# Two 64-row score products in turns instead of one 128-row product of stacked copies, in a two-layer trunk step

## The chip, the cores and the metric

The program runs on one core of one Trainium2 chip. The metric is the device time of one execution in microseconds (us). Every time below is such a time, or is read from one profiled execution of the kernel before.

## What is computed

One step of a hybrid trunk with two layers, 1024 features, 512 sample tokens and 128 prompt tokens. Each layer runs three mixers side by side (differential attention, a chunkwise mLSTM, a spatial gate), merges them by gates, and then runs a gated feed-forward network. The change is in the attention. A head has a query and a key of 128 features, which are two halves of 64, and each half has a softmax of its own:

```
q1, q2 = qblk[..., :DA_HD], qblk[..., DA_HD:]          # DA_HD = 64
p1 = softmax(einsum('bhqd,bhkd->bhqk', q1, k1) * scale)
p2 = softmax(einsum('bhqd,bhkd->bhqk', q2, k2) * scale)
o  = einsum('bhqk,bhkv->bhqv', p1 - lam * p2, v)
```

There are four heads. A block is 128 queries. The four sample blocks read 640 keys (512 of the sample, 128 of the cache); the prompt block reads its own 128.

## The kernel before

Activations lie with their features on the 128 partitions and the 640 tokens (`NT`) along the free dimension. A large product is made of pieces of 320 tokens. Each float32 operand of such a product is split exactly into a high and a low part of type float32r, and a product is the sum of three terms: high by high, high by low, low by high (line 129 for most of the kernel). So one column tile of a weight with eight row tiles is 48 products of 128x128 by 128x320. Each product loads its own stationary operand (the rows of PEld) and then streams its columns (the rows of PE).

The scores use another split. `attn_stacks` makes, for each half j of a head, one tile `qs` that holds the high part of q on 64 partitions and the low part on the other 64, a tile `kh` that holds the high part of k twice, and a tile `kl` that holds its low part twice. Then two products over all 128 rows, with `kh` and with `kl`, give the whole sum. `attn_weights` (line 826) does this for a block: for j = 0 four products into one accumulator (two terms, two pieces of 320 keys; line 840), the maximum (line 845), its scaling (846), the exponential (848); then the same for j = 1; then the difference of the two softmaxes (850 to 854). `attn_apply` turns that difference (862), copies it (864), multiplies it by v (869) and takes the result out of PSUM (870 on VectorE, 872 on ScalarE).

The prompt block goes by line 843: one plain float32 product for each half, on 64 partitions. A plain float32 product appears in the profile as two passes.

All accumulators of this part come from one tag of PSUM with two slots (`psM`, tag `ms`): in the order of the program j = 0, j = 1, then the turned weights of the block before (862), then its result (869), and so on. `attn_head` goes through the prompt block and then the four sample blocks, and applies each block after the scores of the next one. The tiles of `attn_stacks` have the tag `st`, with six slots; a head takes all six.

The order of the instructions on each engine is fixed when the program is built, by a planner (`schedule_with_timeline_sim=True`) that works through the instructions by priority. An attention head is traced under `high_priority()`; the products of line 129 that are traced around it (`mlstm_out`, `branch`, the gates) are ordinary work, and stand between the head's instructions on TensorE.

Of the kernel before, what the change touches and what calls it, by code (L numbers as in the profile page):

```python
# [9 lines left out]
F32 = mybir.dt.float32  # L10
# [6 lines left out]
P = 128  # L17
D = 1024
KD = D // P
NS = 512  # L20
# [4 lines left out]
# the token blocks of a half, and the halves' columns by conditioning (sample 0, prompt 1)  # L25
NPARTS = ((0, P), (P, 2 * P), (2 * P, NHALF))
GROUPS = (((0, NHALF, 0),), ((NHALF, NS, 0), (NS, NT, 1)))
# steps of the covering products before a norm's sums and before their broadcast
COVER = (4, 8)
# steps by which the second of two products that share a new norm lags, for each half  # L30
LAG = (2, 6)
# idle products at the start that keep TensorE's clock up
# [9 lines left out]
# output tiles of the mLSTM branch between the attention heads  # L42
FILL_ML = (0, 2, 4, 8)
# slots of the attention branch's gates that are made before the last head is through
AHEAD = ("qk", "qk", "tg", "tg", "hs")
# the hidden tiles that are summed in one go
FFN_PARTS = ((0, 7), (7, 14), (14, 22))

# columns of the per-layer vector pack
V_DAG, V_MLG, V_FB, V_IB, V_SGG = 0, 1, 2, 3, 4  # L50
V_MCW, V_MCB, V_FCW, V_FCB, V_BMOD, NV = 8, 32, 40, 172, 216, 264
# tile order of the feature-major part of w_in
# [4 lines left out]
class Tags:  # L57
    """A pool with a number of slots for each tag."""
# [8 lines left out]
class Trunk:  # L67
# [9 lines left out]
    # ---------------------------------------------------------------- helpers  # L77
    def psA(self):
        """A 640-column product over two banks; its halves are split at token 320."""
        return self.t(self.ps, [P, 1024], F32, "acc", 2)[:, 192:832]  # L80
# [4 lines left out]
    def alt(self):  # L85
        """VectorE and GpSimd in turns, for work that either can do."""
        self.flip += 1
        return self.nc.gpsimd if self.flip % 2 else self.nc.vector

    def weights(self, src, n):  # L90
        """Loads a chunk and splits it exactly into two float32r parts, 512 columns at a time."""
        nc = self.nc
        raw = self.t(self.wp, [P, n], F32, "raw")
        nc.sync.dma_start(raw, src)
        out = []
        for a in range(0, n, 512):
            b = min(a + 512, n)
            hi = self.t(self.wp, [P, b - a], F32R, "whi")
            lo = self.t(self.wp, [P, b - a], F32R, "wlo")
            nc.scalar.copy(hi, raw[:, a:b])  # L100
            self.alt().tensor_sub(lo, raw[:, a:b], hi.bitcast(F32))  # L101
            out.append((hi, lo))
        return out
# [13 lines left out]
    def mm(self, acc, w, k0, xs, halves=(0, 1), ks=None, pin=False):  # L117
        """acc[m, t] = sum_k w[k, m] x[k, t]; w holds the tiles k0.. of len(xs)."""
# [21 lines left out]
    def tm(self, l, kind, xs, evac):  # L140
        """Token-major product with 512 columns of w_in, 256 columns at a time. Blocks that share a bank
        of the accumulator start it once."""
# [27 lines left out]
    # ---------------------------------------------------------------- set-up  # L170
    def consts(self):
# [8 lines left out]
        # silu of the two conditionings, padded to 32 columns  # L180
# [23 lines left out]
    def layer_consts(self, l):  # L204
# [11 lines left out]
        # tensors of the mixers  # L216
# [29 lines left out]
    def mod_part(self, l, sec, c0, width, src, pin=False):  # L246
        """Columns c0.. of one of the six modulation vectors, as [feature, (sample, prompt)]."""
        self.mod_vector(*self.mod_products(l, sec, c0, width, src, pin))

    def mod_products(self, l, sec, c0, width, src, pin=False):  # L250
        """Rows 32 j and 32 j + 1: the parts that every fourth feature tile gives."""
# [42 lines left out]
    # ---------------------------------------------------------------- norms  # L294
    def norm_open(self, l, sec, pool, tag):
        """A norm is made for one half of the tokens, then for the other. Without sec: the final one."""
        return {"l": l, "sec": sec, "pool": pool, "tag": tag, "acc": [None, None], "u": {}}

    def feed(self, st, k, x, s):
        """Sums the squares of half s of feature tile k, and scales it."""  # L300
# [15 lines left out]
        if k == KD - 2 and s == 0:  # L316
            # has the square root's table in place when the sum is ready
            nc.scalar.activation(self.t(self.sp, [P, 1], F32, "warm", 1), sq[:, 0:1], AF.Sqrt)

    def norm_sums(self, st, s):  # L320
        """The means of squares of half s, as columns in PSUM; the inverse roots."""
# [12 lines left out]
    def norm_bcast(self, st):  # L334
        """The inverse roots on every partition, in PSUM."""
# [7 lines left out]
    def norm_tiles(self, st, s, out):  # L343
        """Half s of the normed tiles, in two parts, added to out."""
# [37 lines left out]
    def start(self, p0):  # L382
        """The first norm, and two products that begin with the half of its features that is there first."""
# [12 lines left out]
        def warm(n):  # L396
            """Keeps TensorE's clock up while it waits."""
# [51 lines left out]
    def handoff(self, srcs, xs, x, g, st, nexts):  # L449
        """The last two tiles of a residual product, the norm that follows, and the first two products with  # L450
        its result, first for one half of the tokens, then for the other: a half's norm is made while
        TensorE works on the other half."""
# [11 lines left out]
        def cover(accs, ws, xs, half, s, order):  # L464
            """Half of the columns of two products, within them the sums of the norm's half s."""
# [22 lines left out]
        # the second product starts some steps later: its accumulator is the last to be free  # L488
# [13 lines left out]
    # ---------------------------------------------------------------- spatial gating  # L502
# [43 lines left out]
    # ---------------------------------------------------------------- mLSTM  # L546
    def mlstm_in(self, l, h):
        """The gates, and v with a column of ones (token-major)."""
# [27 lines left out]
    def gates(self, l, acc):  # L576
        """Rows: forward heads at partitions 0-3, backward ones at 32-35."""
# [10 lines left out]
        # log sigmoid(f) = min(f, 0) - log(1 + exp(-|f|))  # L588
# [14 lines left out]
        # M: running maximum of a chunk's a and of the exponent of the state it starts from (mp)  # L603
# [54 lines left out]
    def mlstm_head(self, l, h, q, k, v, rows, sums):  # L658
        """Both directions of one head over all chunks."""
# [14 lines left out]
        for d in range(2):  # L674
# [15 lines left out]
            # q scaled by what is left of the incoming state, and that state's decay  # L690
# [42 lines left out]
    def head_norm(self, hs, sums):  # L733
        """RMS over each head's width: the inverse for every (token, head)."""
# [25 lines left out]
    # ---------------------------------------------------------------- attention  # L760
# [14 lines left out]
    def attn_qk(self, l, h, head):  # L775
        """Rotated q and k of the sample; the prompt's are left as they are."""
# [16 lines left out]
    def attn_stacks(self, h, q, k):  # L793
        """For both halves j of a head, over all 128 rows: q's high and low part on top of each other,
        and k's high part twice, and k's low part twice (512 keys of the sample, 128 of the cache).
        Then [qh; ql] . [kh; kh] + [qh; ql] . [kl; kl] is the whole product."""
        nc, p = self.nc, self.p1
        out = []
        for j in range(2):
            a, b = slice(HD * j, HD * j + HD), slice(HD - HD * j, P - HD * j)  # L800
            qs, kh, kl = (self.t(p, [P, NT], F32R, "st") for _ in range(3))
            nc.scalar.copy(qs[a, 0:NS], q[a, 0:NS])
            nc.vector.tensor_sub(qs[b, 0:NS], q[a, 0:NS], qs[a, 0:NS].bitcast(F32))
            for src, c0, c1 in ((k[a, 0:NS], 0, NS), (self.ck[a, h, :], NS, NT)):
                nc.scalar.copy(kh[a, c0:c1], src)
                nc.vector.tensor_sub(kl[a, c0:c1], src, kh[a, c0:c1].bitcast(F32))
            nc.vector.tensor_copy(kh[b, :], kh[a, :].bitcast(F32))
            nc.gpsimd.tensor_copy(kl[b, :], kl[a, :].bitcast(F32))
            out.append((qs, kh, kl))
        return out  # L810

    def attn_head(self, l, h, q, k, v, sums):
        """One head: the weights of a block of queries are made while the block before it is applied."""
        nc, p = self.nc, self.p1
        stacks = self.attn_stacks(h, q, k)
        o = self.t(p, [P, NB, P], F32, "hs")
        before = None
        for b in (NB - 1, 0, 1, 2, 3):
            e = self.attn_weights(b, stacks, q, k)
# [6 lines left out]
    def attn_weights(self, b, stacks, q, k):  # L826
# [6 lines left out]
        es = []  # L833
        for j in range(2):
            ps = self.psM()[:, 192:832]
            if sample:
                st, kh, kl = stacks[j]
                for i, kk in enumerate((kh, kl)):
                    for s in (0, 320):
                        nc.tensor.matmul(ps[:, s : s + 320], st[:, qs], kk[:, s : s + 320], start=i == 0, stop=i == 1)  # L840
            else:
                r = slice(HD * j, HD * (j + 1))
                nc.tensor.matmul(ps[:, 0:P], q[r, qs], k[r, NS:NT], start=True, stop=True)
            mx = self.t(self.sp, [P, 1], F32, "mx", 6)
# [33 lines left out]
    # ---------------------------------------------------------------- branches  # L878
# [6 lines left out]
    def branch(self, l, n, h, ys, merged, ms, first=False, last=False, ahead=None):  # L885
        """merged += (1 + tanh(gate / 2)) * (y @ w_branch[n]), twice the gated sum, for output tiles ms."""
# [20 lines left out]
    # ---------------------------------------------------------------- FFN  # L907
    def ffn(self, l, h, accs, x, p2, nxt):
        """The residual update and the next norm."""
# [26 lines left out]
        for f0, f1 in FFN_PARTS:  # L936
            # the next part's first tile fills the time in which this part's last one is finished
# [20 lines left out]
    # ---------------------------------------------------------------- all of it  # L958
# [82 lines left out]
# ---------------------------------------------------------------------- host  # L1041
def _shape_constants():
    """Identity, masks, selectors and rotary tables: they depend on shapes alone."""
# [18 lines left out]
def _tiles(w):  # L1062
    """[L, K, M] -> [L, M/128, 128, K/128 * 128]: one column tile per chunk."""
# [4 lines left out]
def _columns(v):  # L1068
    """[L, n * 128] -> [L, 128, n]."""
# [72 lines left out]
```

## Time and profile before

| what | value |
|---|---|
| median of 3 timed runs | 2445.26 us (2442.68 to 2446.33) |
| the profiled execution, from its first to its last instruction | 2439.1 us |
| what the median holds beyond that span | 6.2 us |
| TensorE matmuls busy | 2408.0 us, 99% |
| TensorE weight loads busy | 2313.9 us, 95% |
| VectorE, ScalarE, GpSimd busy | 1134.0, 944.8, 669.9 us |
| mean granted TensorE clock | 0.998 of full speed |
| products of line 840 | 256 |

The profile gives for the profiled execution its span and no other time. "Busy" of a matmul runs from its start to a modelled end, and one matmul starts before the one ahead of it ends; so the busy time of a group says less than the distance from start to start, which the chain of waits gives as the time of a piece divided by its count. The chain is followed back from the last instruction; each piece names an engine, a tile, a line and how many instructions it holds.

### The profile page before, as it was taken

The numbers are of one execution on the slowest core, as the hardware profiler recorded it, in microseconds if no ns is written. First come the engines' busy times: TensorE is split into PE (matmuls) and PEld (weight loads), VectorE is DVE, ScalarE is ACT, GpSimd is POOL, SyncE is SP. The second block draws the span as 40 slices with busy tenths as digits, with TensorE's granted clock in tenths as the row PEclk, the third lists the DMA queues.
The fourth block names the chain that finished last, engine by engine and source line by source line (L and its number), as shares of the span: only waits on it lengthen the run. The fifth ranks groups of instructions, "written<-read, shape, count | busy, mean of one in ns | idle before, by whom it ended". The sixth has DMA issues, their size and how long they took to land.

```text
span 2439.1 us, 40662 instructions
## 1 busy us (share of the span) xinstructions
PE 2408.0 (99%) x16708; PEld 2313.9 (95%) x16708; DVE 1134.0 (46%) x2111; ACT 944.8 (39%) x1728; POOL 669.9 (27%) x486
## 2 busy tenths in 40 slices
PE   8999999999999999999999999999999999999998
PEld 7999999999598999999999999999986989999998
DVE  5455545553146433424446455455532454244344
ACT  4433335544145322323454332455442543232334
POOL 2322232332222322313213222323322223232231
PEclk9999999999999999999999999999999999999999
DMA  8221221123544234222322212211233432222222
GB/s 282 74 73 64 65 78 62 60 72 132 173 147 160 69 109 140 72 75 79 103 80 70 74 64 66 76 54 62 97 114 120 147 96 74 79 74 73 81 72 69
DMA packets 88761, 227.39 MB, mean 93 GB/s; under 512 B 9472, under 2 KB 23936, under 8 KB 88576
## 3 DMA queue, kind: packets, MB, share of 16 engines
q1 hardware_dynamic: 88576, 224.80, 28.2%
q8 instruction: 131, 2.15, 0.4%
q14 instruction: 54, 0.44, 0.1%
HBM read 217.41 MB, written 7.35 MB: 92 GB/s over the span
## 4 chain that ended last, share of the span: by engine, by line
PE 96%; DVE 3%; ACT 1%; DMA 0%; issue 0%; SPq 0%; DVEq 0%; POOL 0%; POOLq 0%; ACTq 0%
PE acc L129 77%; PE acc L156 6%; PE ms L264 3%; PE ms L869 2%; PE ms L840 2%; PE ms L156 1%; PE ms L862 1%; PE ms L716 1%; PE ms L718 1%; PE ms L705 1%; DVE x L439 0%; PE ms L670 0%; PE ms L536 0%; PE ms L277 0%; PE ms L327 0%
## 5 line engine op out<-in xcount | busy, mean ns | idle before, releaser
L129 PE MATMUL acc<-h,whi 128*128 128x320 f32 x6464 | 1246.9, 311 | 5.0 <-DVE h L356 3.3
L129 PEld LDWEIGHTS acc<-h,whi 128*128 128x128 f32 x6464 | 1019.3, 188 | 32.1 <-issue 19.3
L100 ACT CAST whi<-raw 128x512 fp32r<-128x512 f32 x596 | 365.3, 614 | 1038.1 <-PE acc L129 787.9
L101 POOL TENSOR_TENSOR wlo<-raw,whi 128x512 fp32r<-128x512 f32 (+1 forms) x298 | 390.7, 1311 | 1355.1 <-ACT whi L100 1304.7
L129 PE MATMUL acc<-h,wlo 128*128 128x320 f32 x3232 | 755.4, 310 | 0.0
L129 PEld LDWEIGHTS acc<-h,wlo 128*128 128x128 f32 x3232 | 544.2, 188 | 3.5 <-issue 3.4
L101 DVE TENSOR_TENSOR wlo<-raw,whi 128x512 fp32r<-128x512 f32 (+1 forms) x298 | 241.2, 810 | 451.0 <-ACT whi L100 435.0
L129 PE MATMUL acc<-act,whi 128*128 128x320 f32 x1408 | 269.6, 310 | 0.0
L129 PEld LDWEIGHTS acc<-act,whi 128*128 128x128 f32 x1408 | 222.0, 188 | 4.2 <-issue 2.5
L129 PE MATMUL acc<-act,wlo 128*128 128x320 f32 x704 | 165.5, 309 | 0.0
L129 PE MATMUL acc<-y,whi 128*128 128x320 f32 x768 | 154.3, 314 | 1.7 <-DVE y L114 1.7
L499 DVE SCALAR_TENSOR_TENSOR x<-acc,mod,x 128x128 f32<-128x128 f32 (+3 forms) x136 | 66.3, 527 | 181.3 <-PE acc L129 181.3
L165 DVE SCALAR_TENSOR_TENSOR cw<-acc,vec,cw 128x511 f32<-128x511 f32 (+1 forms) x176 | 95.7, 544 | 115.1 <-ACT cw L163 114.0
L156 PE MATMUL acc<-whi,h 128*128 128x256 f32 x768 | 145.7, 283 | 0.0
L129 PEld LDWEIGHTS acc<-y,whi 128*128 128x128 f32 x768 | 121.2, 188 | 17.3 <-issue 11.7
L156 PEld LDWEIGHTS acc<-whi,h 128*128 128x128 f32 x768 | 123.0, 192 | 0.0
L129 PEld LDWEIGHTS acc<-act,wlo 128*128 128x128 f32 x704 | 119.1, 188 | 0.0
L916 POOL TENSOR_TENSOR cw<-cw,cw 128x640 f32<-128x640 f32 x44 | 69.2, 1573 | 156.5 <-DVE cw L167 151.9
L156 PE MATMUL acc<-wlo,h 128*128 128x256 f32 x384 | 108.7, 283 | 0.0
L167 DVE SCALAR_TENSOR_TENSOR cw<-acc,vec,cw 128x511 f32<-128x511 f32 (+1 forms) x176 | 96.7, 550 | 6.0
L129 PE MATMUL acc<-y,wlo 128*128 128x320 f32 x384 | 92.1, 315 | 0.0
L848 ACT ACTIVATE wk<-ms,mx 128x640 f32<-128x640 f32 (+1 forms) x80 | 56.7, 709 | 76.6 <-DVE mx L846 73.2
(257 smaller groups left out, 2425.0 us busy)
## 6 DMA issues: line engine op xcount, KB each, us to landing
raw<-w_in_f SPq DMA_DIRECT2D x98, 512.0 KB, 3.4
raw<-w_up SPq DMA_DIRECT2D x88, 512.0 KB, 3.3
wk<-w_mod SPq DMA_DIRECT2D x72, 256.0 KB, 3.4
mw<-w_mod SPq DMA_DIRECT2D x72, 256.0 KB, 5.7
raw<-w_down SPq DMA_DIRECT2D x32, 448.0 KB, 3.3
raw<-w_in_v SPq DMA_DIRECT2D x24, 512.0 KB, 3.7
raw<-w_branch SPq DMA_DIRECT2D x24, 512.0 KB, 3.3
mw<-w_mod SPq DMA_DIRECT2D x16, 512.0 KB, 8.8
```

Source lines behind the costliest of these rows:

```text
L100: nc.scalar.copy(hi, raw[:, a:b])
L101: self.alt().tensor_sub(lo, raw[:, a:b], hi.bitcast(F32))
L129: ins = nc.tensor.matmul(acc[:, s], a[:, sl], b[:, s], start=k == 0 and i == 0, stop=k == last and i == 2)
L156: nc.tensor.matmul(accs[b], a[:, bs], w[:, sl], start=first and b % 2 == 0, stop=last and (b % 2 == 1 or b == NB - 1))
L165: nc.vector.scalar_tensor_tensor(dst[:, a + 1 : b], acc[:, a : b - 1], w0, dst[:, a + 1 : b], ALU.mult, ALU.add)
L167: nc.vector.scalar_tensor_tensor(dst[:, a : b - 1], acc[:, a + 1 : b], w2, dst[:, a : b - 1], ALU.mult, ALU.add)
L264: ins = nc.tensor.matmul(ps[j : j + 32, 0:width], self.cs[:, k, :], raws[k], start=k < 4, stop=k >= 4, tile_position=(0, j))
L499: self.nc.vector.scalar_tensor_tensor(x[:, a:b], acc[:, a:b], g[:, k, i : i + 1], x[:, a:b], ALU.mult, ALU.add)
L840: nc.tensor.matmul(ps[:, s : s + 320], st[:, qs], kk[:, s : s + 320], start=i == 0, stop=i == 1)
L848: nc.scalar.activation(e[:, 0:nk], ps[:, 0:nk], AF.Exp, bias=mx, scale=scale, accum_out=sm[:, j : j + 1])
L869: nc.tensor.matmul(po, at[:, c * P : (c + 1) * P], vv, start=c == 0, stop=c == n - 1)
L916: nc.gpsimd.tensor_mul(cs[0], cs[0], cs[1])
```

## The change

`attn_stacks` is replaced by `attn_parts`, which splits q and k of a head once, with both halves in place on their own 64 partitions: four tiles `qh`, `ql`, `kh`, `kl` instead of six, and six instructions instead of sixteen. `attn_weights` takes both accumulators of a sample block first and then makes twelve products of 64 rows: three terms, two pieces of 320 keys, and for each of these j = 0 (partitions 0 to 63) and j = 1 (partitions 64 to 127) in turns. The maxima and exponentials of the two halves follow after that. The rest of the diff removes comments and docstrings.

```
-    def attn_stacks(self, h, q, k):
+    def attn_parts(self, h, q, k):
         nc, p = self.nc, self.p1
-        out = []
-        for j in range(2):
-            a, b = slice(HD * j, HD * j + HD), slice(HD - HD * j, P - HD * j)
-            qs, kh, kl = (self.t(p, [P, NT], F32R, "st") for _ in range(3))
-            nc.scalar.copy(qs[a, 0:NS], q[a, 0:NS])
-            nc.vector.tensor_sub(qs[b, 0:NS], q[a, 0:NS], qs[a, 0:NS].bitcast(F32))
-            for src, c0, c1 in ((k[a, 0:NS], 0, NS), (self.ck[a, h, :], NS, NT)):
-                nc.scalar.copy(kh[a, c0:c1], src)
-                nc.vector.tensor_sub(kl[a, c0:c1], src, kh[a, c0:c1].bitcast(F32))
-            nc.vector.tensor_copy(kh[b, :], kh[a, :].bitcast(F32))
-            nc.gpsimd.tensor_copy(kl[b, :], kl[a, :].bitcast(F32))
-            out.append((qs, kh, kl))
-        return out
+        qh, ql, kh, kl = (self.t(p, [P, NT], F32R, "st") for _ in range(4))
+        nc.scalar.copy(kh[:, 0:NS], k[:, 0:NS])
+        nc.scalar.copy(qh[:, 0:NS], q[:, 0:NS])
+        nc.scalar.copy(kh[:, NS:NT], self.ck[:, h, :])
+        nc.vector.tensor_sub(kl[:, 0:NS], k[:, 0:NS], kh[:, 0:NS].bitcast(F32))
+        nc.vector.tensor_sub(ql[:, 0:NS], q[:, 0:NS], qh[:, 0:NS].bitcast(F32))
+        nc.gpsimd.tensor_sub(kl[:, NS:NT], self.ck[:, h, :], kh[:, NS:NT].bitcast(F32))
+        return qh, ql, kh, kl
...
-        es = []
-        for j in range(2):
-            ps = self.psM()[:, 192:832]
-            if sample:
-                st, kh, kl = stacks[j]
-                for i, kk in enumerate((kh, kl)):
-                    for s in (0, 320):
-                        nc.tensor.matmul(ps[:, s : s + 320], st[:, qs], kk[:, s : s + 320], start=i == 0, stop=i == 1)
-            else:
+        pss = [self.psM()[:, 192:832] for _ in range(2)]
+        if sample:
+            qh, ql, kh, kl = parts
+            for i, (x, y) in enumerate(((qh, kh), (qh, kl), (ql, kh))):
+                for s in (0, 320):
+                    for j, ps in enumerate(pss):
+                        r = slice(HD * j, HD * (j + 1))
+                        nc.tensor.matmul(ps[:, s : s + 320], x[r, qs], y[r, s : s + 320], start=i == 0, stop=i == 2)
+        else:
+            for j, ps in enumerate(pss):
                 r = slice(HD * j, HD * (j + 1))
                 nc.tensor.matmul(ps[:, 0:P], q[r, qs], k[r, NS:NT], start=True, stop=True)
+        es = []
+        for j, ps in enumerate(pss):
             mx = self.t(self.sp, [P, 1], F32, "mx", 6)
```

## Rows read from the trace of the kernel before

**Rows 1.** The page: span, TensorE's busy time, the chain by line.

```profile
span 2439.1 us, 40662 instructions
...
PE 2408.0 (99%) x16708; PEld 2313.9 (95%) x16708; DVE 1134.0 (46%) x2111; ACT 944.8 (39%) x1728; POOL 669.9 (27%) x486
...
PE acc L129 77%; PE acc L156 6%; PE ms L264 3%; PE ms L869 2%; PE ms L840 2%; PE ms L156 1%; PE ms L862 1%; PE ms L716 1%; PE ms L718 1%; PE ms L705 1%; DVE x L439 0%; PE ms L670 0%; PE ms L536 0%; PE ms L277 0%; PE ms L327 0%
```

**Rows 2.** Groups of instructions, shapes apart: the scores' products (busy, mean ns).

```profile
L840 PE MATMUL ms<-st,st 128*128 128x320 f32 x256 | 52.0, 319 | 2.4 <-DVE st L807 2.3
```

**Rows 3.** The chain, a long unbroken piece (start us, us, what xcount).

```profile
340.04 17.62 PE acc L129 x120
```

**Rows 4.** The chain in a sample block of the first head, and in the last block.

```profile
392.79 1.12 PE ms L869 x10
393.91 0.59 PE ms L840 x4
394.50 4.10 PE acc L129 x28
398.60 0.58 PE ms L840 x4
399.18 1.17 PE acc L129 x8
...
1780.92 0.59 PE ms L840 x4
1781.51 3.08 PE acc L129 x21
1784.59 0.58 PE ms L840 x4
```

**Rows 5.** Timeline of VectorE and ScalarE behind the first of these blocks.

```profile
394.14 0.28 DVE L870 COPY hs<-ms 128x128 f32<-128x128 f32 x1
...
395.00 0.26 ACT L872 ACTIVATE osq<-ms 128x128 f32<-128x128 f32 x1
395.15 0.19 ACT L872 ACTIVATION_READ_ACCUMULATOR osq<-ms 128x1 f32 x1
```

**Rows 6.** The chain from the prompt block of the second head.

```profile
416.43 0.42 PE ms L843 x4
416.85 5.33 PE acc L129 x35
422.18 0.30 PE ms L840 x2
422.48 1.32 PE acc L129 x9
423.80 0.58 PE ms L840 x4
424.38 1.90 PE acc L129 x13
426.29 0.30 PE ms L840 x2
```

**Rows 7.** The chain from the prompt block of the third head.

```profile
471.70 0.22 PE ms L869 x2
471.93 0.42 PE ms L843 x2
472.34 1.09 PE ms L869 x8
473.43 5.28 PE acc L129 x36
478.71 0.42 PE ms L843 x2
479.13 0.78 PE acc L129 x4
```

**Rows 8.** Lines 843 and 869: durations ns min/median/max, first and last start.

```profile
L843 PE MATMUL ms<-qk,qk x32: 272/322/373, 358.0 to 1745.4; 64*128 64x128 f32 x32
...
L869 PE MATMUL ms<-lc,wk x64: 275/275/275, 383.1 to 1797.3; 128*128 128x128 f32 x64
```

**Rows 9.** The first head: TensorE's busy time in 358 to 416; two timeline rows.

```profile
358.00:416.00 58.00, 56.82 (x407) 56.16 (x407) 34.93 (x70) 33.04 (x70) 12.91 (x10) 1.00 0.16 52
...
362.37 0.56 PE L840 MATMUL ms<-st,st 128*128 128x320 f32 x2
...
364.06 0.83 PE L840 MATMUL ms<-st,st 128*128 128x320 f32 x4 [1.14 <-DVE st L807]
```

**Rows 10.** Lines of `attn_stacks` on VectorE and GpSimd: durations ns min/median/max.

```profile
L803 DVE TENSOR_TENSOR st<-qk,st x16: 685/906/1095, 352.2 to 1743.8; 64x512 fp32r<-64x512 f32 x16
...
L806 DVE TENSOR_TENSOR st<-qk,st x16: 671/686/1660, 360.2 to 1744.9; 64x512 fp32r<-64x512 f32 x16
...
L807 DVE CAST st<-st x16: 486/488/492, 360.9 to 1746.8; 64x640 fp32r<-64x640 f32 x16
...
L808 POOL CAST st<-st x16: 714/964/1043, 361.0 to 1746.9; 64x640 fp32r<-64x640 f32 x16
```

More of the change, by code (lines that the diff above doesn't have):

```diff
@@ L791, in attn_qk @@
         return qk
-    def attn_stacks(self, h, q, k):
+    def attn_parts(self, h, q, k):
         nc, p = self.nc, self.p1
-        out = []
-        for j in range(2):
-            a, b = slice(HD * j, HD * j + HD), slice(HD - HD * j, P - HD * j)
-            qs, kh, kl = (self.t(p, [P, NT], F32R, "st") for _ in range(3))
-            nc.scalar.copy(qs[a, 0:NS], q[a, 0:NS])
-            nc.vector.tensor_sub(qs[b, 0:NS], q[a, 0:NS], qs[a, 0:NS].bitcast(F32))
-            for src, c0, c1 in ((k[a, 0:NS], 0, NS), (self.ck[a, h, :], NS, NT)):
-                nc.scalar.copy(kh[a, c0:c1], src)
-                nc.vector.tensor_sub(kl[a, c0:c1], src, kh[a, c0:c1].bitcast(F32))
-            nc.vector.tensor_copy(kh[b, :], kh[a, :].bitcast(F32))
-            nc.gpsimd.tensor_copy(kl[b, :], kl[a, :].bitcast(F32))
-            out.append((qs, kh, kl))
-        return out
+        qh, ql, kh, kl = (self.t(p, [P, NT], F32R, "st") for _ in range(4))
[6 more added lines that the diff above has]
+        return qh, ql, kh, kl
     def attn_head(self, l, h, q, k, v, sums):
         nc, p = self.nc, self.p1
-        stacks = self.attn_stacks(h, q, k)
+        parts = self.attn_parts(h, q, k)
         o = self.t(p, [P, NB, P], F32, "hs")
@@ L818, in attn_head @@
         for b in (NB - 1, 0, 1, 2, 3):
-            e = self.attn_weights(b, stacks, q, k)
+            e = self.attn_weights(b, parts, q, k)
             if before is not None:
@@ L824, in attn_head, with attn_weights @@
         return o
-    def attn_weights(self, b, stacks, q, k):
+    def attn_weights(self, b, parts, q, k):
         nc, p = self.nc, self.p1
```

## Prediction

> **What bounds the kernel now.** I read the page first, then the groups of instructions, then the chain of waits through the attention, and last the timeline of single instructions. TensorE is busy for 99% of the span, and nearly the whole chain is TensorE's, three quarters of it line 129 [rows 1]. So what counts is the time that TensorE's own sequence takes; what VectorE, ScalarE or GpSimd save pays only where TensorE waits for them. The price of a product is read from an unbroken piece of the chain: 120 products in 17.62 us, 0.147 us from start to start for 320 columns [rows 3]. (The mean of 319 ns in [rows 2] is the modelled length of one, and overlaps its neighbours.) Line 840 pays the same, four in 0.59 us [rows 4]. Its 256 products are 256 x 0.147 = 37.6 us of the span; this is all that the change can touch on TensorE.
>
> **Where the scores stand in TensorE's order.** In a sample block the four products for j = 0 come right behind the block before's line 869; then come 28 products of line 129; only then the four for j = 1 [rows 4]. This pattern, two groups with other work between them, holds for blocks 1 to 3 of all eight heads (24 blocks; j = 1 comes 4.7 us behind j = 0 in the first shown and 3.7 in the last). The reason is the two slots of `ms`. The slot for j = 0 is the one that line 864 has emptied; the slot for j = 1 is that of line 869's result, which lines 870 and 872 empty some time after 869 ends (at about 395.3, 1.4 us after 393.91 [rows 4, 5]). The planner does not let TensorE stand for it: it takes the next instruction that is ready, whatever its place in the program. Its own picture of that release is later still, since j = 1 stands at 398.60.
>
> **What 64-row products cost.** The kernel has some already, line 843. In the second head both halves stand side by side: four passes take 0.42 us of the chain [rows 6]. In the third head they stand apart, and the two passes of one half alone take 0.42 us as well [rows 7]. So a partner in the other half of the array is free, and a half alone is paid in full. A pass itself is no cheaper for having 64 rows: 272 ns recorded for those that don't wait, 275 for a 128-row pass of line 869 [rows 8]. But two passes of 869 take 0.22 us, so 0.20 of the 0.42 is not product. And what follows is long too: eight passes of 869 take 1.09 us where ten take 1.12 (0.20 too much), 35 products of line 129 take 5.33 where 35 x 0.147 = 5.13 (0.20 too much), four take 0.78 for 0.59 [rows 4, 6, 7]. Going from 128-row to 64-row products and back costs about 0.40 us, for each group, in all the places I looked at.
>
> The Trainium skill has this rule on the page "TensorEngine Tiling (Array Packing)", Key Properties: changing the tiling mode, not just the tile, drains TensorE. The trace agrees, and adds the price of 0.40 us that the page doesn't give; without such a price the sum below would be 27 us lower.
>
> **The change part by part.**
>
> Removed: 256 products, -37.6 us.
>
> Added: 384 products of 64 rows by 320 columns in one pass. None is in the trace; from below each costs 0.073 us (every one with a partner), from above 0.147 (alone). The text puts the halves in turns, but what the planner sees is which of them is ready. In blocks 1 to 3, when j = 0's slot is free, j = 1's isn't; the next instruction that is ready is j = 0's second piece, and so on through all six. They need 0.88 us, less than the 1.4 us until the other slot is empty even as the chip runs. So I take two groups of six alone: 12 x 0.147 = 1.76 us in place of 1.17, +0.59 a block. In block 0 both slots come free together if line 843's two halves stood together, which they do in the first two heads of each layer [rows 6] and don't in the other two [rows 7]. So 4 blocks pair (6 x 0.147 = 0.88) and 28 don't (1.76): 3.5 + 49.3 - 37.6 = +15.2 us.
>
> Added: the way in and out, 0.40 us for each group. Blocks 1 to 3 have two groups: 48. Block 0 now comes in three or four pieces, as its operands get ready [rows 6]; this was free among 128-row products and no longer is. I take two for the paired ones and three for the others, since the operands come from six instructions: 4 x 2 + 4 x 3 = 20. 68 x 0.40 = +27.2 us. The bounds: 32 groups (one a block) is 12.8, 88 (five in each block 0) is 35.2; and if only what is lost behind a group counted, 0.20 each, 68 are 13.6.
>
> The preparation: per head VectorE loses two each of lines 803, 806 (twice) and 807, and gains two subtractions over 128 partitions with the same 512 columns, which I take at line 803's 0.9 us; about 3.4 us saved, and GpSimd has a subtraction of 128 columns in place of two copies of 0.96 [rows 10]. Nearly all is hidden already: TensorE idles only 1.18 us of the first head's 58 us, waiting for line 807 between 362.9 and 364.06 [rows 9]. That can go, in both layers: -2.4 us. If it didn't, the cost is those 2.4. GpSimd's piece of `kl` may come late and split a group: counted above.
>
> The later maximum of j = 0, by up to a microsecond, moves line 862 back; line 129's products fill the place, as they do now.
>
> Sum: 15.2 + 27.2 - 2.4 = +40.0 us. The span of 2439.1 becomes 2479.1; with the 6.2 us that the median holds beyond it, 2485 us.
>
> **The rivals.**
>
> *The halves do pair.* The planner might get both slots at one time, if the copy out of 869 counts as short. Then 32 x 0.88 - 37.6 = -9.4 us; groups 24 + 16 = 40, +16.0; idle -2.4: +4.2 us, 2449. For it: line 843 pairs in two heads of four, though nothing in the text asks for it. Against it: 24 blocks in which j = 1 stands microseconds later. 18%.
>
> *Apart, but the change of shape is cheap for these products* (a float32r product streams in one pass, line 843 takes two): 15.2 - 2.4 = +13 us, 2458, or up to 2472 with half the price. Against it: the 0.20 us behind a group falls on 129's one-pass products. 8%.
>
> *Faster: paired, with the shape changed for less.* A paired block saves 0.29 us of products, so the change wins as soon as way in and out cost less than 0.29 us a block in one group. At nothing: -9.4 - 2.4 = -12 us, 2433. Against it are all groups of [rows 6, 7]. 6%. The same page's section Theoretical Speedup gives up to 2x for products of at most 64 rows; taken alone it leads to this time. The trace agrees on the 2x within a pair.
>
> *More pieces than I count*, five and more in each block 0, or groups broken in blocks 1 to 3 too: with 88 groups, no pairs and no idle time regained 15.2 + 3.5 + 35.2 = +54 us, 2499 and more. 6%.
>
> **How the numbers follow.** The forecast, halves apart at 0.40 us a group, has 62%; its own range is 2478 to 2496 (50 to 88 groups, the idle time regained at the one end and not at the other). The time predicted is 2485 us. For 8 in 10 the range also takes in the cheap change of shape and the upper half of the paired case: 2449 to 2499. What a measurement of this kernel can tell from no change is about 0.2%, 4.9 us: "same" is 2440.4 to 2450.2. Half of the paired case lies there: 0.10 with a little of the others. Faster has 0.07, slower 0.83.
>
> **What would show it.** In the chain of the changed kernel: the products of 64 rows in groups of six behind line 869, with some 20 of line 129 before the next six, right if so; groups of twelve that take about 1.1 us would prove me wrong on the order. A group of six should take 1.08 us of the chain (0.88 + 0.20) and the work behind it 0.20 more than its products. TensorE's pause at 363 should shrink. The prediction is wrong if the groups number nearer 32 than 68, if the price of a group is not near 0.40 us, or if a partner is not free for products of 320 columns.

## The result and the profile after

The changed kernel takes 2483.01 us (median of four runs, 2480.61 to 2485.47) against 2445.44 us before (four runs, 2442.68 to 2446.33): a ratio of 1.0158, 95% interval 1.0144 to 1.0173, or 37.6 us more. 2485 was predicted.

The page of the changed kernel (span, busy time of each engine) shows the same kind of kernel as before: TensorE is busy for 99% of the span [rows 1]. TensorE has 128 more products, and VectorE, ScalarE and GpSimd have a little less to do, which buys about 2 us (below).

```profile
span 2483.7 us, 40806 instructions
...
PE 2453.7 (99%) x16836; PEld 2338.7 (94%) x16836; DVE 1114.6 (45%) x2063; ACT 935.7 (38%) x1704; POOL 660.6 (27%) x478
```

The line numbers have moved: the scores' products are line 835 (840 before), the prompt's 839 (843), the transposes 860 (862), the product with the values 867 (869). The groups of instructions, shapes apart, show the new products (busy, mean ns | idle time before them); their mean length is that of the 128-row products [rows 2]:

```profile
L835 PE MATMUL ms<-st,st 64*128 64x320 f32 x384 | 69.9, 324 | 0.0
```

The chain of the changed kernel (start us, us, what xcount): the piece of 120 products that opens the attention, two sample blocks of the first head, and the end of the first layer's attention.

```profile
343.76 17.62 PE acc L129 x120
...
398.28 1.12 PE ms L867 x10
399.39 1.07 PE ms L835 x6
400.46 3.57 PE acc L129 x23
404.03 1.09 PE ms L835 x6
405.12 1.66 PE acc L129 x10
...
602.34 18.18 PE acc L129 x124
620.52 1.98 PE ms L264 x16
```

This is the pattern that the prediction described, beside [rows 4]: two groups of six, apart, 23 products of line 129 between them. Six products would take 0.88 us at 0.147; each group takes 1.07 or 1.09, so 0.20 more. The 23 products behind the first take 3.57 instead of 3.38, the 10 behind the second 1.66 instead of 1.47: 0.19 more each.

The piece of 120 products takes 17.62 us in both kernels [rows 3], and it opens the attention in both, so the stage can be measured from it to the first products of line 264, the modulation behind the attention: 620.52 - 343.76 = 276.76 us here. Before, the same two marks stand at 340.04 and 598.25, 258.21 us:

```profile
598.25 1.98 PE ms L264 x16
```

The second layer shows the same two lengths within 0.1 us. So the attention has grown by 18.55 us a layer, 37.1 us in all, which is nearly the whole of the measured 37.6.

The profiled spans differ by more, 44.6 us. The execution profiled after the change was the longest of its four, and it had a few stretches with the clock at half that the one before didn't have; the windows (stretch, length, busy time of each engine, granted clock, DMA share, GB/s) show one of them, 8 us at 0.57 behind the second attention, where before has 1.00:

```profile
1994.00:2002.00 8.00, 7.75 (x35) 7.37 (x39) 5.86 (x17) 3.26 (x9) 0.00 (x0) 0.57 0.21 66
```

### The profile page after: what moved, and what is told of

Its sections match the earlier page's. It is cut to its first block, busy times and chain, and to the rows that moved or that the text cites. A ratio compares the mean times of both kernels' runs of the same rounds, so it can differ in the third digit from the quotient of the medians.

```text
span 2483.7 us, 40806 instructions
## 1 busy us (share of the span) xinstructions
PE 2453.7 (99%) x16836; PEld 2338.7 (94%) x16836; DVE 1114.6 (45%) x2063; ACT 935.7 (38%) x1704; POOL 660.6 (27%) x478
## 4 chain that ended last, share of the span: by engine, by line
PE 96%; DVE 2%; ACT 1%; issue 0%; DMA 0%; SPq 0%; POOL 0%; DVEq 0%; ACTq 0%; POOLq 0%
PE acc L129 77%; PE acc L156 6%; PE ms L264 3%; PE ms L835 3%; PE ms L867 2%; PE ms L156 1%; PE ms L860 1%; PE ms L716 1%; PE ms L718 1%; PE ms L705 1%; PE ms L670 0%; PE ms L536 0%; PE ms L277 0%; PE ms L327 0%; DVE x L439 0%
## 5 line engine op out<-in xcount | busy, mean ns | idle before, releaser
L843 DVE TENSOR_REDUCE mx<-ms 128x1 f32<-128x640 f32 (+1 forms) x80 | 56.5, 715 | 80.0 <-PE ms L835 79.8
```

Of the source, the lines that this page charges most:

```text
L843: nc.vector.tensor_reduce(mx, ps[:, 0:nk], axis=AX.X, op=ALU.max)
```

## The experiments

The theory (T) is that of the prediction: products that stand apart, plus some 0.40 us for every group that changes the shape of the products, both on TensorE's own sequence. The rivals (R) are named in each expectation. For each kernel the table has the median, the ratio to the kernel before with its interval, and the first layer's attention, measured in the trace from the start of the last product of the values (line 156) to the start of the first of line 264. The marks used above give 0.2 us less. Between these marks lie 1392 products of line 129 in each of the eight kernels, so the stage holds the same other work in all. Each ratio is to the runs of the kernel before that were taken for it; their median is 2445.44 us for the changed kernel, 2443.75 for the next three and for the prompt scores, 2442.71 for the other two.

| kernel | us | ratio | attention, us |
|---|---|---|---|
| before | 2445.44 | | 258.43 |
| after | 2483.01 | 1.0158 [1.0144, 1.0173] | 276.97 |
| products of 128 rows, twelve a block | 2460.25 | 1.0069 [1.0055, 1.0083] | 266.07 |
| products of 128 rows, eight a block | 2444.53 | 0.9999 [0.9990, 1.0007] | 257.33 |
| both accumulators awaited | 2500.29 | 1.0236 [1.0222, 1.0250] | 284.09 |
| awaited in one head only | 2475.98 | 1.0137 [1.0121, 1.0152] | 270.49 |
| before, prompt scores of 128 rows | 2442.48 | 0.9997 [0.9988, 1.0006] | 257.87 |
| before, modulation not split | 2409.27 | 0.9866 [0.9846, 0.9886] | 258.43 |

**The shape alone.** The changed kernel, with its products over all 128 rows; the order of the instructions on each engine stays (in the traces only one spot in the third head differs, where the first two of a block stand in turns with the prompt's passes in the changed kernel).

```
-  nc.tensor.matmul(ps[:, s : s + 320], x[r, qs], y[r, s : s + 320], start=i == 0, stop=i == 2)
+  nc.tensor.matmul(ps[:, s : s + 320], x[:, qs], y[:, s : s + 320], start=i == 0, stop=i == 2)
```

> The changed kernel with one thing undone: the twelve products of a block read all 128 rows of q and k instead of 64 (so each half's scores get the other half's added, which leaves the arithmetic wrong and the work the same in count, order and columns). The instructions stand in the same order on every engine. If the price lies in the change of the array's shape, about 62 groups lose about 0.39 us each (-24.4 us), and the four blocks that ran in pairs lose their partners (+3.5 us): about 2462 us. If the price lies in the number of products and in their weight loads, and the shape is free, nothing is saved and the pairs are lost: 2483 to 2487 us.

2460.25 us. The chain of this kernel in the same two blocks:

```profile
394.38 1.12 PE ms L867 x10
395.49 0.88 PE ms L835 x6
396.37 3.37 PE acc L129 x23
399.74 0.88 PE ms L835 x6
400.62 1.46 PE acc L129 x10
```

Same order, same counts, and all four surcharges are gone: 0.88 instead of 1.07 and 1.09, 3.37 instead of 3.57, 1.46 instead of 1.66. The attention is 10.9 us a layer shorter, 21.8 in all. Two blocks a layer that pair in the changed kernel (below) can't pair here and pay 0.88 more each, 3.5 us. And a wait of the changed kernel, in the first head of each layer, is not in this one (who waits for whom: us in all, times, longest us):

```profile
PE acc L129 <- ACT tg L754: 0.9, 2, 0.5
```

So the shape costs 21.8 + 3.5 - 0.9 = 24.4 us over 62 groups, 0.39 us each. The rival, that groups standing apart are the whole price, falls.

**The preparation alone.** The kernel of the last experiment with eight products a block instead of twelve, as many as before. What is left of the change is its preparation and the order in the text.

```
-  for i, (x, y) in enumerate(((qh, kh), (qh, kl), (ql, kh))):
+  for i, (x, y) in enumerate(((qh, kh), (ql, kl))):
 ...
-  nc.tensor.matmul(ps[:, s : s + 320], x[:, qs], y[:, s : s + 320], start=i == 0, stop=i == 2)
+  nc.tensor.matmul(ps[:, s : s + 320], x[:, qs], y[:, s : s + 320], start=i == 0, stop=i == 1)
```

> As the run before, with two terms instead of three (high by high and low by low, over all 128 rows; the cross terms are left out): eight products of 128 rows a block, as many as the kernel before had, but with the changed preparation, both accumulators taken first, and both maxima behind all products. If these changes beside the products cost nothing, the time is that of the kernel before less some of TensorE's idle time at the first head: 2443 to 2446 us. If the preparation or the later maximum cost anything, it shows here alone: above 2450 us.

2444.53 us, no difference that can be measured from before, and its chain is that of [rows 4] again, with four products in 0.59 us:

```profile
394.56 0.59 PE ms L835 x4
...
399.10 0.58 PE ms L835 x4
```

The attention is 1.1 us a layer shorter than before, so the lighter preparation and the later maximum together give 2.2 us. Of this 1.6 us is idle time of TensorE in the first head: 1.18 us a layer before [rows 9], 0.39 here. Between this kernel and the last lie 64 products a layer and 8.74 us; the last has no idle time there, so the products cost 9.13 us, 0.143 each, where 0.147 was reckoned.

**Pairs forced.** The changed kernel, but the first product of a block waits until the last result has been copied and squared out of its accumulator, so that both accumulators are free when the six of the first half begin.

```
+  def after_evac(self, ins):
+      dep = mybir.DependencyInfo(mybir.DependencyClass.Sync, mybir.DependencyReason.DATA)
+      for e in self.evac:
+          self.tc.add_manual_dep(ins.ins, e.ins.name, dep, reason="both slots")
+      self.evac = ()
 ...
-  nc.tensor.matmul(ps[:, s : s + 320], x[r, qs], y[r, s : s + 320], start=i == 0, stop=i == 2)
+  ins = nc.tensor.matmul(ps[:, s : s + 320], x[r, qs], y[r, s : s + 320], start=i == 0, stop=i == 2)
+  self.after_evac(ins)
 ...
-  nc.vector.tensor_copy(o[:, b, :], po)
+  cp = nc.vector.tensor_copy(o[:, b, :], po)
 ...
+  self.evac = (cp, sq)
```

> The changed kernel, where the first product of a block also waits until the results of the block before have been taken out of PSUM, so that both accumulators are free at once. In the order that is built, all 32 blocks are one group of twelve and the prompt's products one pair. If a partner is free for products of 320 columns, a group takes 1.08 us of the chain and TensorE's own work comes to that of the kernel before within 2 us. But a block's softmax no longer runs beside the other half's wait, the heads take more of line 129's products as cover, and none are left between the last three blocks of each layer's last head: TensorE will stand there for some 3 us a block, about 20 us in all, so 2458 to 2475 us. If products of 320 columns didn't overlap, a group would take 1.96 us and the time be above 2485 us.

2500.29 us, slower than the changed kernel: a miss. All 32 blocks now stand in one group of twelve, and the pairing itself is real. The chain of this kernel (its added lines shift the scores to 842, the product with the values to 875, the transposes to 868) in a block of the first head, and in the last head:

```profile
377.29 1.07 PE ms L842 x12
...
590.70 1.19 PE ms L842 x11
...
597.20 2.52 PE ms L875 x10
...
599.74 0.30 DVE hs L876
...
600.06 0.38 ACT osq L878 x2
...
600.48 2.01 PE ms L842 x12
602.49 1.54 DVE mx L851 x2
...
607.80 2.52 PE ms L875 x10
```

Twelve products take 1.07 us, as long as six alone: the partner costs nothing. But the wait lasts, and other products must fill it. In the last head none are left. Result, copy, square, scores and maximum then follow each other in the chain without a product of line 129 between them, and one block's ten passes of line 875 (five products) come 10.6 us behind the last block's (597.20, 607.80). The windows of this kernel there (same columns):

```profile
589.00:625.00 36.00, 20.54 (x101) 17.05 (x100) 10.61 (x26) 12.48 (x29) 0.00 (x0) 0.56 0.22 66
```

TensorE is busy for 20.5 of 36 us, and the granted clock is 0.56: once TensorE had begun to stand, the clock fell to its lower level (1.2 GHz) for most of this stretch. The chain prices it: the scores take 1.19 us at 590.70 and 2.01 at 600.48, and ten passes of line 875 take 2.52 us, where the same ten took 1.12 in the changed kernel. The expectation had the cover run out at about 3 us a block; a block without cover took 10.6 us, of which its own products at full clock are 2.7 (1.07 scores, 1.12 values, 0.55 transposes), so some 8 are lost. Pairs were tested here together with a wait, so the time says nothing against pairs.

**Pairs in one head.** The same wait, in the third head of each layer only, where products of line 129 are left to fill it.

```
+  self.wait = h == 2
 ...
-  for e in self.evac:
+  for e in self.evac if self.wait else ():
```

> The changed kernel with the wait for both accumulators in the third head of each layer alone. In the order that is built, that head's four sample blocks are one group of twelve each and its prompt products one pair, 5 groups in place of 11, and enough of line 129's products are left to cover it. Four blocks less 0.88 us of products and six groups less at 0.40 us: -5.9 us a layer. The attention of a layer, from the last product of its values to the first modulation product behind it, goes from 277.0 to about 271 us, and the time from 2483 to about 2471 us. If pairing gave nothing, or the waits cost as much as they did with all heads waiting, it stays at 2483 us or above.

2475.98 us, where about 2471 was expected. The chain of this kernel in two blocks of that head (scores line 844, values 877), and just behind the attention:

```profile
488.69 1.07 PE ms L844 x11
...
502.61 1.07 PE ms L844 x11
...
610.20 1.13 PE ms L877 x10
...
612.13 1.28 ACT L738
...
614.82 1.88 DVE hs L741
```

(The chain lists eleven of the twelve; the timeline has all.) In the attention the wait gives 6.5 us a layer, 13 in all, a little more than the 5.9 a layer expected: in the fourth head, too, the first group of scores now follows the prompt's products at once, one group less. In this head pairs do pay, since they also stop its first block from falling to pieces. But the covering products were spent there. Behind the attention 8 of line 129 are left, where the changed kernel has 124 (its chain at 602.34): ScalarE and VectorE appear in the chain, TensorE waits for the norm and the next products' operands, and the stretch between the two attentions is 4.3 us longer than after. By the two medians 7 us of 13 remain; by the distance from the kernel before, 37.6 us after and 33.3 here, only 4. The kernel is still 33 us slower than before.

**The old kernel's own shape change.** The kernel before computes its prompt scores with 64-row products, line 843. Here they have 128 rows, from a tile that holds one half of the keys and zeros in the other.

```
+  self.kz = self.t(lp, [P, 2, P], F32, "kz", 1)
+  nc.gpsimd.memset(self.kz, 0.0)
 ...
+  nc.gpsimd.tensor_copy(self.kz[r, j, :], x[r, NS:NT])
 ...
-  nc.tensor.matmul(ps[:, 0:P], q[r, qs], k[r, NS:NT], start=True, stop=True)
+  nc.tensor.matmul(ps[:, 0:P], q[:, qs], self.kz[:, j, :], start=True, stop=True)
```

> The kernel before, with its only 64-row products (the prompt block's scores) made 128-row ones: the keys of a half with zeros in the other half's rows. If each group of 64-row products costs 0.40 us beside its products, eight lone halves save 0.40 us each and four pairs 0.18 us each (they lose the partner): -3.9 us, about 2441.5 us. If the shape is free: four pairs lose 0.22 us each, 2446 us.

2442.48 us, no measurable difference; the attention is 0.56 us a layer shorter where 1.95 was expected. The waits of TensorE's weight loads over the whole kernel (who waits for whom: us in all, times, longest us):

```profile
PEld ms L845 <- ACT wk L852: 3.0, 6, 0.6
PEld acc L129 <- ACT tg L756: 2.9, 4, 0.8
```

Before, the waits that answer to these two come to 0.6 us in two cases (for line 848) and 2.7 in two (for line 754), so there are six more waits and 2.6 us more of waiting. Of these 2.6 us 0.5 stand in the first heads of the two layers and the rest in the third and fourth, where the kernel before has no such wait. TensorE's own idle time in the attention has grown by 0.5 us a layer, from 1.18 to 1.67. So waiting is a part, perhaps the most, of what lacks of the 3.9 us expected for both layers, of which 1.1 came. The order moved with the edit, so the waits can't be put down to one part of it, and this run is inconclusive.

**Where the kernel before splits its groups.** If each group in another shape is paid for its way in and out, such a group should not be split. Line 264 has such products: eight to a result, four at a time in four 32-column strips of the array, two passes each, so that a whole result is an x16 in the chain. The planner splits them. In the chain of the kernel before, behind the attention:

```profile
612.49 1.85 PE ms L264 x16
...
618.49 0.97 PE ms L264 x2
619.46 0.34 PE acc L129
...
625.21 0.98 PE ms L264 x4
```

One product standing alone (x2) costs 0.97 us, two side by side (x4) 0.98, and all eight in one piece (x16) 1.85. Here the products of a 512-column section are issued in reverse order of their weights, so that the product whose weights land last comes first, and the other seven are ready behind it.

```
-  for k in range(KD):
+  back = width == 512
+  for k in reversed(range(KD)) if back else range(KD):
 ...
-  start=k < 4, stop=k >= 4,
+  start=(k >= 4) == back, stop=(k < 4) == back,
```

> The kernel before, with the other place in which products of a part of the array are split up: the modulation products (line 264, 32 columns wide, four of them side by side in the array) take their eight loads in reverse, so that the first product waits for the last load and the eight stand together. Behind the first layer's attention 26 of these now go in 23 groups, 0.97 us and 0.19 us behind each for lone ones; together eight take 1.85 us and 0.19. That is 26.7 us against 6.6, -20 us for the layer and about as much for the second: 2405 us. What the loads then hold up (11.6 MB pass in this stretch) would take a part of it back: 2405 to 2430 us. If lone products cost only their columns, nothing is gained: 2444 us or more, since the first product waits longer.

2409.27 us, 33 us faster than the kernel before and 74 faster than the changed one. The chain of this kernel (line 265 is the others' 264):

```profile
615.47 1.85 PE ms L265 x16
...
621.48 4.40 PE acc L129 x30
625.88 1.85 PE ms L265 x16
```

Single products with line 129 between them have become whole results of 1.85 us. The attention itself keeps its 258.43 us; the stretch between the attentions is 14.2 us shorter, the one behind the second 16.9, of the 20 expected for each. By the expectation's own sum most of this comes from the partners that a lone product lacks: 23 x 0.97 = 22.3 us against 3.25 x 1.85 = 6.0. The 0.19 us behind each group, 23 times against 3.25, is only 3.8 of the 20. The run doesn't separate the two.

## Why the prediction was right

The two kernels with 128 rows split the attention's +37.1 us into the prediction's terms: the steps are before to eight products, eight to twelve, twelve to after. TensorE's idle time in the first head differs between the four kernels (1.18, 0.39, 0.00 and 0.47 us a layer), so it is taken out of each step and has a row of its own.

| term | predicted | measured | from |
|---|---|---|---|
| pause regained | -2.4 | -1.4 | idle time after, less before |
| preparation beside it | 0 | -0.6 | eight products of 128 rows, less before |
| products apart | +15.2 | +14.7 | 18.3 from eight to twelve, less 3.5 of pairs |
| shape changed | +27.2 | +24.4 | after less twelve of 128 rows, pairs taken out |
| sum | +40.0 | +37.1 | |

**The halves stand apart: right.** In blocks 1 to 3 of all heads the six of one half stand alone as [rows 4, 5] had it, and forcing them together showed that a partner would have been free.

**A free partner and a half paid in full: right.** Six alone take 1.07 to 1.09 us; in the second head of the changed kernel the first sample block pairs, and its group takes no longer (its chain; eleven of twelve listed):

```profile
428.00 1.08 PE ms L835 x11
429.08 5.62 PE acc L129 x37
```

**0.40 us a group: right, 0.39.** It is a price of the group and not of its products: two alone cost 0.48 us for 0.29 (below), six alone 1.07 for 0.88, twelve in pairs 1.07 for 0.88, and what follows any of them costs 0.19 or 0.20 more. Without this term the change would cost some 13 us, as the rival of the cheap shape had it. The Trainium skill's rule on the page "TensorEngine Tiling (Array Packing)", Key Properties, that a change of the tiling mode drains TensorE, agrees with this; the figure is the runs'.

**68 groups: too many, 62.** I took two groups for block 0 of the first two heads and three for the others. The first two have one (428.00 above for the second head, 365.97 below for the first). In the fourth head it is two of six. In the third it is four, of which one is joined to the prompt's products and pays no way of its own (chain of the changed kernel, third head and then fourth):

```profile
485.99 0.30 PE ms L839
486.30 0.05 PE ms L835
486.34 0.07 PE ms L839
486.41 0.08 PE ms L835
486.49 0.34 PE acc L129
486.83 0.48 PE ms L835 x2
487.31 0.49 PE acc L129 x2
487.80 0.49 PE ms L835 x2
488.29 3.42 PE acc L129 x22
491.71 1.09 PE ms L835 x6
...
548.09 1.07 PE ms L835 x6
...
552.43 1.09 PE ms L835 x6
```

Two products that stand alone here cost 0.48 us, where 0.29 is product. The count is 31 net groups a layer. Six too many at 0.40 is 2.4 of the 2.9 us by which the sum is too high; the other differences are 0.4 or 0.5 us each and partly cancel.

**The pause: half right.** The wait for line 807 is gone, as expected; in the place of those 1.14 us [rows 9] TensorE waits once for ScalarE, 0.47 us, behind the paired group of the first head. So 1.4 us of the 2.4 come back in the two layers. That the preparation as a whole gives 2.0, near the 2.4, is luck: the other 0.6 was not forecast, and its cause stays open. In the timeline of the changed kernel:

```profile
365.97 1.17 PE L835 MATMUL ms<-st,st 64*128 64x320 f32 x12
367.61 0.85 PE L129 MATMUL acc<-h,whi 128*128 128x320 f32 x4 [0.47 <-ACT tg L754]
```

**The time beyond the span: the wrong account, without harm.** I added 6.2 us to the span as if every run had them. An execution has only some 2 us beyond its span: 2485.47 against 2483.7 for the one profiled after, and 2440.88 against 2439.1 for a run of the kernel before with the span of the profiled one. So the other 4.4 us mean that the execution profiled before was a short one among its kind. The sum was right since it came out at the median before plus 40.0; between medians, the attention's 37.1 us is nearly all of the 37.6.

The rival of pairs everywhere, at 2449, was wrong in its order: pairs come only where both accumulators happen to be free. The two kernels that force them show that the price of making them free is covering work, which the rival left out. The rival on the other side needed a shape change under 0.29 us; it is 0.39. The rival of more pieces needed 88 groups; there are 62.

## What to carry to other kernels

Count the groups that change the shape of the products in the order that TensorE really runs, not in the order of the text, and price each from a place in the old trace where that shape already stands: here 0.40 us a group outweighed the products themselves. Filling an empty half of the array saves time only if its accumulator is free at the same moment and the group is long: a paired block saves 0.29 us of products here and pays 0.39. The same count turned the other way found a gain: keeping whole the groups that already have another shape made the old kernel 33 us faster, most of it, by the expectation's sum, since lone products had no partners.

## What the runs showed that was not expected

- A lone strip is paid like four: one product in a strip of 32 columns costs 0.97 us of the chain, two side by side 0.98, and eight, as two rounds of four, 1.85.
- When TensorE ran out of cover, the clock made it worse: at a granted clock of 0.56 over 36 us, the same ten passes took 2.52 us instead of 1.12, and since these products are themselves what VectorE and ScalarE wait for there, the next wait grew with them.
- Where two halves pair, the single-pass products of the new lines and the two-pass ones of the prompt can share a stretch: in the third head the passes of lines 839 and 835 alternate within 0.50 us (the four rows at 485.99).
